# Wider gate-value products, low parts by accumulating transfers, and a shorter end chain in a two-layer decoder trunk on Trainium2

## Chip, cores and metric

The kernel runs on one core of a Trainium2 chip. The metric is the device time of one execution in microseconds (us), as a median over runs. A profile of one execution, taken by the hardware profiler, shows what the core's engines did: TensorE (PE, with its weight loads PEld), VectorE (DVE), ScalarE (ACT), GpSimd (POOL), SyncE (SP), and the transfer (DMA) queues.

## What is computed

Two layers; each adds a mixer and a gated feed-forward to the residual h (512 tokens, width 1024, all in float32). The mixer's input projection yields u and v of a spatial gate and q, k, v of a differential attention. Cut to what matters here:

```python
for l in range(DEPTH):
    n = rmsnorm(h, attn_norm[l])
    u, v_sgu, q, k, v_att = jnp.split(n @ w_in[l], [512, 1024, 1536, 2048], axis=-1)
    u, v_sgu = jax.nn.gelu(u), jax.nn.gelu(v_sgu)
    y_sgu = sgu_mixer(u, v_sgu, ...)   # v normed in 4 groups of 128, mixed over chunks of 128 tokens
    y_att = diff_attention(q, k, v_att, positions, ...)   # 4 heads, rotary on q and k
    h = h + jnp.concatenate([y_sgu, y_att], axis=-1) @ w_out[l]
    h = h + conv_ffn(rmsnorm(h, ffn_norm[l]), ...)        # the larger part of the products
return rmsnorm(h, final_norm)
```

## The kernel before

**Numbers and products.** Every factor of a product is split into a high part (float32 rounded to the type fp32r) and a low part (the value minus its high part, again fp32r). A product is three on TensorE: high x high, high x low, low x high. The activations lie with features on the partitions, 8 tiles of 128 x 512 tokens. `feat_gemm` keeps the weights stationary and moves 512 tokens; its output has features on the partitions. `tok_gemm` keeps 128 tokens stationary and moves weights, 256 columns at a time; its output has tokens on the partitions (the values of the attention and the gate values need this). Two token tiles share a PSUM bank there.

**Weights** come in blocks of 128 x 1024 float32 (512 KB), in a fixed order (`specs`), 96 a layer; of a layer's blocks 0 to 19 are `w_in`: gate values (first half), q of heads 0 and 1, gate values (second half), k, v, q, k, v of the other heads, u. `block(i)` (L156) issues what is needed up to two blocks ahead: a load by SyncE into `raw`, the high part by ScalarE (`act.copy`, L167), the low part by a subtraction (L173), on GpSimd in two halves of 512 columns for the blocks of the mixer after the first seven, on VectorE or GpSimd in the rest. `raw`, `wh` and `wl` have three buffers each.

**Order.** In the mixer the order of instructions on each engine is written out by hand: `Ordered` (L114) chains each instruction to the one before it on its engine. Instructions issued past that wrapper (`nc.sync`, `nc.vector`, `nc.gpsimd`) are set by the planner. The products are generators that yield after each step; `run` takes steps, and after each step one item from the list `due`, in which the work on results is queued (rotary products, gelus, norms, splits).

**Mixer of a layer.** Forty steps come before the attention's loop: in layer 0 gate values and q together as the inputs arrive (`both_first`, 16 steps, from the blocks that `opening` loads piece by piece), the second gate values, k, v; in layer 1 gate values, q, gate values, k, v. Then the loop runs over 16 units (4 heads x 4 query tiles) and two more; each unit has scores, exponentials, difference, transpose, split, product with the values, each some units behind the other, and between these the remaining steps of `products` are run (q, k, v of heads 2 and 3, u). `later` holds items that are done one per unit; in layer 0 these are the last k part, the masks of the spatial weights (`spatial`) and the norm of the second half of the gate values (sums, root, `normed`, `part`). GpSimd does the rotary products of q and k and the subtractions. `rsqrt` is a chain of 11 small VectorE operations.

**PSUM** has four banks for products, two for scores, two for transposes. The gate values of layer 0's second half use the scores' banks.

**End.** The last products (`dl`) run over halves of 256 tokens. For each output tile `squares` adds its square to `acc_last`; `columns` transposes the sums with TensorE, adds them up and takes the root; `result` spreads the roots over the partitions by TensorE into two banks (`sc_last`, copied by ScalarE to `rstd_last` for GpSimd, and `sr_last`, read by VectorE), multiplies and stores by SyncE. The second half's chain stands alone behind the last product.

## Time and profile before

| | |
|---|---|
| median of 3 runs (lowest to highest) | 1132.91 us (1132.48 to 1134.14) |
| profiled execution | 1133.84 us |
| its span, first to last instruction | 1132.1 us |
| TensorE busy | 1115.3 us, 99% |
| VectorE busy | 691.0 us, 61% |
| ScalarE busy | 478.1 us, 42% |
| GpSimd busy | 412.9 us, 36% |
| transfer queue of SyncE | 104.27 MB, 29.1% of 16 engines |

The shares are means over stages: the mixers take about 5 to 205 us and 566 to 759 us of the span, the feed-forwards the rest. A busy TensorE is not one at its peak, since pipelined products overlap in the timeline; the distance from the start of one to the start of the next is what counts. In a row of the timeline or of the groups, `out<-in` are the program's names of the tiles, and what stands behind the last arrow is what ended the idle time before. Nearly all rows have line L119, the wrapper that records every operation, so tiles tell them apart.

### The profile page before, as it was taken

The numbers are of one execution on the slowest core, as the hardware profiler recorded it, in microseconds if no ns is written. First come the engines' busy times: TensorE is split into PE (matmuls) and PEld (weight loads), VectorE is DVE, ScalarE is ACT, GpSimd is POOL, SyncE is SP. The second block draws the span as 40 slices with busy tenths as digits, with TensorE's granted clock in tenths as the row PEclk, the third lists the DMA queues.
The fourth block names the chain that finished last, engine by engine and source line by source line (L and its number), as shares of the span: only waits on it lengthen the run. The fifth ranks groups of instructions, "written<-read, shape, count | busy, mean of one in ns | idle before, by whom it ended". The sixth has DMA issues, their size and how long they took to land.

```text
span 1132.1 us, 14943 instructions
## 1 busy us (share of the span) xinstructions
PE 1115.3 (99%) x5637; PEld 936.4 (83%) x5637; DVE 691.0 (61%) x1271; ACT 478.1 (42%) x810; POOL 412.9 (36%) x390
## 2 busy tenths in 40 slices
PE   9998999999999999999999999999999999999996
PEld 7987888888888888888899788888888888888886
DVE  7779874775763237664347887767657522666634
ACT  6453653544442124443344554454444312444351
POOL 0466233533232103432556742453313310332351
PEclk9999999999999999999999999999999999999999
DMA  8221122232333333223332221122332323322322
GB/s 272 76 79 65 45 65 94 95 101 90 105 94 95 92 112 93 93 84 94 103 110 81 87 74 57 56 94 93 96 109 94 97 91 110 93 94 93 88 80 75
DMA packets 34215, 105.24 MB, mean 93 GB/s; under 512 B 4064, under 2 KB 8544, under 8 KB 34144
## 3 DMA queue, kind: packets, MB, share of 16 engines
q1 hardware_dynamic: 33712, 104.27, 29.1%
q8 instruction: 44, 0.72, 0.3%
q14 instruction: 27, 0.22, 0.1%
q10 hardware_dynamic: 432, 0.03, 0.0%
HBM read 102.19 MB, written 2.10 MB: 92 GB/s over the span
## 4 chain that ended last, share of the span: by engine, by line
PE 87%; DVE 9%; ACT 2%; issue 1%; POOL 1%; DVEq 0%; ACTq 0%; POOLq 0%
PE g L119 21%; PE v L119 20%; PE dn L119 19%; PE wo L119 7%; PE u L119 4%; PE vs L119 3%; PE q L119 3%; PE dl L119 3%; PE av L119 1%; PE sc L119 1%; PE k L119 1%; PE mx L119 1%; DVE s L119 1%; ACT wh L119 1%; PE va L119 1%
## 5 line engine op out<-in xcount | busy, mean ns | idle before, releaser
L119 POOL TENSOR_TENSOR wl<-raw,wh 128x512 fp32r<-128x512 f32 x187 | 256.2, 1391 | 565.1 <-ACT wh L119 546.8
L119 ACT CAST wh<-raw 128x1024 fp32r<-128x1024 f32 (+1 forms) x192 | 194.2, 1015 | 375.7 <-issue 180.3
L119 DVE TENSOR_TENSOR wl<-raw,wh 128x1024 fp32r<-128x1024 f32 (+1 forms) x96 | 121.2, 1263 | 132.1 <-ACT wh L119 132.0
L119 PE MATMUL v<-gh_f,wh 128*128 128x512 f32 x352 | 137.3, 390 | 0.0
L119 PE MATMUL v<-gl_f,wh 128*128 128x512 f32 x352 | 137.0, 389 | 0.0
L119 PE MATMUL v<-gh_f,wl 128*128 128x512 f32 x352 | 137.0, 389 | 0.0
L119 PE MATMUL g<-gh_f,wl 128*128 128x512 f32 x352 | 136.9, 389 | 0.0
L119 PE MATMUL g<-gh_f,wh 128*128 128x512 f32 x352 | 136.9, 389 | 0.0
L119 PE MATMUL g<-gl_f,wh 128*128 128x512 f32 x352 | 136.9, 389 | 0.0
L119 DVE SCALAR_TENSOR_TENSOR cv<-up_cv,par,cv 128x512 f32<-128x512 f32 x88 | 74.0, 885 | 6.4 <-ACT cv L119 6.1
L119 PEld LDWEIGHTS g<-gh_f,wh 128*128 128x128 f32 x352 | 66.1, 188 | 13.8
L119 PEld LDWEIGHTS v<-gh_f,wh 128*128 128x128 f32 x352 | 66.1, 188 | 13.7
L119 PEld LDWEIGHTS v<-gh_f,wl 128*128 128x128 f32 x352 | 66.1, 188 | 13.7
L119 PEld LDWEIGHTS g<-gh_f,wl 128*128 128x128 f32 x352 | 66.1, 188 | 13.7
L119 PEld LDWEIGHTS g<-gl_f,wh 128*128 128x128 f32 x352 | 66.1, 188 | 13.6
L119 PEld LDWEIGHTS v<-gl_f,wh 128*128 128x128 f32 x352 | 66.1, 188 | 13.5
L119 DVE SCALAR_TENSOR_TENSOR cg<-up_cg,par,cg 128x512 f32<-128x512 f32 x88 | 69.6, 841 | 6.0 <-ACT cg L119 5.6
L119 DVE TENSOR_TENSOR up_cv<-v,rstd_f 128x512 f32<-128x512 f32 x44 | 30.2, 692 | 67.2 <-PE v L119 67.2
L119 ACT ACTIVATE s<-s,mn 128x128 f32<-128x128 f32 (+3 forms) x64 | 35.5, 556 | 72.8 <-DVE mn L119 67.5
L119 DVE TENSOR_TENSOR up_cg<-g,rstd_f 128x512 f32<-128x512 f32 x44 | 30.0, 692 | 57.8 <-PE g L119 54.9
L119 DVE TENSOR_TENSOR hT<-dn,hT 128x512 f32<-128x512 f32 x28 | 19.1, 691 | 46.5 <-PE dn L119 46.5
L119 ACT ACTIVATE cg<-cg 128x512 f32<-128x512 f32 x44 | 27.7, 630 | 45.8 <-DVE cg L119 45.8
(604 smaller groups left out, 2618.4 us busy)
## 6 DMA issues: line engine op xcount, KB each, us to landing
raw<-in_w_up SPq DMA_DIRECT2D x88, 512.0 KB, 3.5
raw<-in_w_dn SPq DMA_DIRECT2D x40, 512.0 KB, 3.5
raw<-in_w_in SPq DMA_DIRECT2D x36, 512.0 KB, 3.4
raw<-in_w_out SPq DMA_DIRECT2D x16, 512.0 KB, 3.4
hT<-in_xT SPq DMA_DIRECT2D x8, 256.0 KB, 4.3
or<-in_w_in SPq DMA_DIRECT2D x16, 128.0 KB, 4.4
raw<-in_w_dn SPq DMA_DIRECT2D x8, 256.0 KB, 3.5
out<-y SPq DMA_DIRECT2D x8, 256.0 KB, 2.2
```

Source lines behind the costliest of these rows:

```text
L119: return lambda *args, **kw: pin(getattr(self.engine, op)(*args, **kw))
```

## The change

Three parts.

1. **Gate values.** All 512 columns at once: `tok_wide` moves 512 columns for each token tile, into four banks (two of the scores', two of the products'). The blocks are built from pieces of two old ones. In layer 0 the opening multiplies the gate values alone (its first k in two halves of 256 columns) and q follows as an ordinary product; in layer 1 gate values, then q. The work behind them is done per token tile: gelu, squares and sums, one root over 16 columns for all, `normed`, `part`. Two tiles are normed before the loop, two in it. `spatial` stands ahead of the loop's last 12 steps in both layers, and the rotary products of the first k are put at the front of `due`.
2. **Low parts.** For blocks 10 to 19 of each layer (q, k, v of heads 2 and 3, and u) ScalarE writes the negated high part to `lo` (scale -1, rounded), a transfer issued by GpSimd adds `raw` onto it, and ScalarE writes the high part. The subtractions on GpSimd for these blocks go.
3. **End.** The square of the last tile is transposed by itself; the sum of the others is turned and added up during the last products (k = 7). The bank that VectorE reads is filled before that which ScalarE copies, and stores alternate between SyncE's and ScalarE's queue.

```diff
-        specs += [a["w_in"][l, c] for c in range(20)]
+        w = a["w_in"][l]
+        specs += [[w[c + k // 4][:, k % 4 * 256 : k % 4 * 256 + 512] for c in (0, 4)] for k in range(0, KD, 2)]
+        specs += [w[c] for c in [2, 3] + list(range(6, 20))]
...
     def block(i):
...
+            i_l = j % (len(specs) // DEPTH)
+            if 10 <= i_l < 20:
+
+                act.activation(lo, raw, AF.Identity, scale=-1.0)
+                nc.gpsimd.dma_start(out=lo, in_=raw.bitcast(F32R), accum_op=ALU.add)
+                act.copy(h, raw)
+                loaded.append((h, lo))
+                continue
             act.copy(h, raw)
-            i_l = j % (len(specs) // DEPTH)
             eng = gps if (j > 6 and i_l != 27 if i_l < 28 else j % 3 == 1) else dve
...
+    def tok_wide(banks, xs, ws=None):
+
+        for k, x in enumerate(xs):
+            if ws:
+                w = ws[k]
+            else:
+                if k % 2 == 0:
+                    h, lo = next_block()
+                c = slice(k % 2 * S, k % 2 * S + S)
+                w = h[:, c], lo[:, c]
+            if ws and k == 0:
+
+                for c in (slice(0, 256), slice(256, S)):
+                    outs = [(t, b[:, c], c.start == 0, False) for t, b in enumerate(banks)]
+                    tok_step(outs, x, [p[:, c] for p in w], True, False)
+                    yield
+                continue
+            for t in (0, 2):
+                tok_step([(t + i, banks[t + i], True, True) for i in range(2)], x, w, k == 0, k == len(xs) - 1)
+                yield
...
             if hp == 0:
 
                 later.appendleft(turned.pop())
-                turned = [f for f in turned if f is not nothing]
-            due.extend(turned)
+                due.extendleft(reversed(turned))
+            else:
+                due.extend(turned[:2] + [nothing] * 2 + turned[2:])
...
         def products():
-            if l == 0:
-                yield from both_first()
-                banks = value_banks(1, sc_bank)
-                yield from tok_gemm(banks, xs)
-                g = gate_work(1, banks)
-                due.extend(g[:2])
-                later.extend([lambda: (spatial(), g[2](), g[3]())] + g[4:])
-            else:
-                yield from gate_values(0)
-                yield from queries(0)
-                yield from gate_values(1)
+
+            banks = [sc_bank(f"vs{t}_{l}") for t in range(2)] + [mm_bank(f"vs{t}_{l}") for t in (2, 3)]
+            yield from tok_wide(banks, xs, first if l == 0 else None)
+            gelu, sums, root, normed, part = gate_work(banks)
...
+            due.extend(([nothing] * 4 if l == 0 else []) + [of(gelu, 2, 3), of(gelu, 0, 1)])
+            q = query_banks(0)
+            yield from feat_gemm(q, xs)
+            turn0, turn1, part0, part1 = rope(q, qs, 0, "q")
+            due.extend([turn0, turn1, of(sums, 0, 1), of(sums, 2, 3), part0, part1, root])
+            due.extend(of(f, t) for f in (normed, part) for t in range(2))
+
+            later.extend(of(f, t) for f in (normed, part) for t in (2, 3))
...
-        if l > 0:
-            spatial()
+        spatial()
         run(steps, 12)
...
+        if m == KD - 1 and cs.start > 0:
+            last_sq.append(sq)
+        elif m > 0:
             (dve if m > 5 else gps).tensor_add(acc[:, cs], acc[:, cs], sq)
...
+        if th == 1:
+            s7 = sums("ss_end", last_sq[0])
+            dve.scalar_tensor_tensor(ss, s7, 1.0 / D, ss, op0=ALU.mult, op1=ALU.add)
         act.activation(r, ss, AF.Sqrt)
...
-        for b in (other, bank):
+        for b in (bank, other):
...
-            nc.sync.dma_start(out=out[m : m + 2, :, cs].rearrange("m p s -> p m s"), in_=y.rearrange("p (m s) -> p m s", m=2))
+            (nc.sync if m % 4 == 0 else nc.scalar).dma_start(out=out[m : m + 2, :, cs].rearrange("m p s -> p m s"), in_=y.rearrange("p (m s) -> p m s", m=2))
...
-    products(1, 3, (0,), lambda: r.append(columns(0)))
-    products(1, 3, (1,), lambda: result(0, r[0]))
-    result(1, columns(1))
+    products(1, 3, (0,), {2: lambda: r.append(columns(0, most(0)))})
+    products(1, 3, (1,), {2: lambda: result(0, r[0]), 7: lambda: r.append(most(1))})
+    result(1, columns(1, r[1]))
```

## Rows read from the trace of the kernel before

**Rows 1.** The page: TensorE's busy time, share, instructions; chain by engine.
```profile
PE 1115.3 (99%) x5637; PEld 936.4 (83%) x5637; DVE 691.0 (61%) x1271; ACT 478.1 (42%) x810; POOL 412.9 (36%) x390
...
PE 87%; DVE 9%; ACT 2%; issue 1%; POOL 1%; DVEq 0%; ACTq 0%; POOLq 0%
```
**Rows 2.** Chain that ended last, in order of time: start us, us, what.
```profile
11.89 1.43 PE vs L119 x12
...
250.29 10.88 PE g L119 x48
...
565.81 11.51 PE vs L119 x96
```
**Rows 3.** Waits of TensorE: who for whom, us in total, times, longest us.
```profile
PE av L119 <- DVE or L389: 3.9, 2, 2.8
...
PE at L119 <- DVE aTl L119: 1.1, 2, 1.0
PE sc L119 <- DVE mn L119: 0.5, 1, 0.5
PE sc L119 <- DVE k_0l L119: 0.3, 1, 0.3
```
**Rows 4.** Windows: length, busy PE, PEld, DVE, ACT, POOL, PEclk, DMA share, GB/s.
```profile
90.00:117.00 27.00, 22.77 (x160) 20.11 (x158) 24.93 (x75) 11.76 (x35) 12.63 (x9) 0.94 0.18 59
117.00:142.00 25.00, 25.00 (x155) 20.88 (x155) 21.44 (x74) 14.02 (x44) 8.43 (x6) 1.00 0.14 44
```
**Rows 5.** Timeline of VectorE: start us, us, instruction, idle before and its end.
```profile
109.51 1.24 DVE L384 TENSOR_SCALAR or<-ssq 128x4 int32<-128x4 int32 x1
110.78 0.17 DVE L385 TENSOR_SCALAR ssq<-ssq 128x4 f32<-128x4 f32 x1
...
112.33 0.42 DVE L119 TENSOR_REDUCE o<-av 128x128 f32<-128x256 f32 x1
```
**Rows 6.** Timeline of GpSimd beside it: two low-part subtractions.
```profile
107.68 3.04 POOL L119 TENSOR_TENSOR wl<-raw,wh 128x512 fp32r<-128x512 f32 x2
```
**Rows 7.** Timeline of TensorE: the product behind its longest wait.
```profile
112.89 0.55 PE L119 MATMUL av<-va,aTh 128*128 128x256 f32 x1 [2.77 <-DVE or L389]
```
**Rows 8.** Timeline before the loop of layer 0: ScalarE and TensorE.
```profile
37.92 1.57 ACT L119 ACTIVATE vs<-vs,rcol_a 128x256 f32<-128x256 f32 x4
...
41.88 0.40 PE L119 MATMUL k<-gh_a,wh 128*128 128x512 f32 x1
...
52.79 0.28 PE L119 MATMUL va<-wh,gh_a 128*128 128x256 f32 x1
...
54.98 1.04 ACT L119 CAST wh<-raw 128x1024 fp32r<-128x1024 f32 x1
...
64.88 0.50 PE L119 MATMUL q<-gh_a,wh 128*128 128x512 f32 x1
```
**Rows 9.** The page: groups (busy, mean ns | idle), DMA issues (KB, us to landing).
```profile
L119 POOL TENSOR_TENSOR wl<-raw,wh 128x512 fp32r<-128x512 f32 x187 | 256.2, 1391 | 565.1 <-ACT wh L119 546.8
...
raw<-in_w_in SPq DMA_DIRECT2D x36, 512.0 KB, 3.4
```
**Rows 10.** Timeline: one issue by SyncE; one rotary product on GpSimd.
```profile
10.93 0.43 SPq L119 DMA_DIRECT2D raw<-in_w_in  x1
...
62.88 1.75 POOL L119 TENSOR_TENSOR k_1sh<-k_1sh,sr 128x512 f32<-128x512 f32 x1
```
**Rows 11.** Timeline of VectorE: root of the second half's gate values, layer 0.
```profile
90.02 1.22 DVE L384 TENSOR_SCALAR gr<-gs 128x8 int32<-128x8 int32 x1
```
**Rows 12.** Chain that ended last, behind TensorE's last product.
```profile
1122.81 0.43 DVE acc_last L119
...
1125.97 0.23 PE sr_last L119 x2
```
**Rows 13.** Timeline of the end: GpSimd's and VectorE's last products.
```profile
1126.53 1.41 POOL L119 TENSOR_TENSOR y<-hT,rstd_last 128x256 f32<-128x256 f32 x2 [5.47 <-ACT rstd_last L119]
...
1127.89 0.41 DVE L119 TENSOR_TENSOR y<-hT,sr_last 128x256 f32<-128x256 f32 x1
```

More of the change, by code (lines that the diff above doesn't have):

```diff
@@ L165, in block @@
             lo = wp.tile([P, 1024], F32R, tag="wl", name=f"wl{j}")[:, :n]
-            (sync if j < 6 else nc.sync).dma_start(out=raw, in_=specs[j])
+            queue = sync if j < 6 else nc.sync
+            if wide:
+                for at, half in enumerate(specs[j]):
+                    o = raw.rearrange("p (k i c) -> p i k c", k=2, i=2)[:, at]
+                    queue.dma_start(out=o, in_=half.rearrange("p (k c) -> p k c", k=2))
+            else:
+                queue.dma_start(out=raw, in_=specs[j])
+            i_l = j % (len(specs) // DEPTH)
[5 more added lines that the diff above has]
+                continue
             act.copy(h, raw)
-            i_l = j % (len(specs) // DEPTH)
             eng = gps if (j > 6 and i_l != 27 if i_l < 28 else j % 3 == 1) else dve
@@ L244, in feat_gemm, with tok_step @@
             yield
-    def tok_step(banks, x, w, first, last):
+    def tok_step(outs, x, w, first, last):
         (xh, xl), (h, lo) = x, w
-        for t in range(NT):
+        for t, o, opens, closes in outs:
             ts = slice(t * P, (t + 1) * P)
-            o = banks[t // 2][:, t % 2 * 256 : t % 2 * 256 + 256]
-            mm(o, xh[:, ts], h, start=first and t % 2 == 0, stop=False)
+            mm(o, xh[:, ts], h, start=first and opens, stop=False)
             mm(o, xh[:, ts], lo, start=False, stop=False)
-            mm(o, xl[:, ts], h, start=False, stop=last and t % 2 == 1)
+            mm(o, xl[:, ts], h, start=False, stop=last and closes)
     def tok_gemm(banks, xs):
+        outs = [(t, banks[t // 2][:, t % 2 * 256 : t % 2 * 256 + 256], t % 2 == 0, t % 2 == 1) for t in range(NT)]
         for k, x in enumerate(xs):
@@ L508, in part @@
                 store[at + j] = split(f"{name}{l}_{at + j}", t1[j])
-            return [partial(turn, 0), partial(turn, 1), nothing, nothing, partial(part, 0), partial(part, 1)]
+            return [partial(turn, 0), partial(turn, 1), partial(part, 0), partial(part, 1)]
         later = deque()
@@ L521, in queries @@
             turned = rope(banks, qs, 2 * hp, "q")
-            due.extend(turned if hp else [f for f in turned if f is not nothing])
+            due.extend(turned[:2] + [nothing] * 2 + turned[2:])
         def keys(hp):
@@ L582, in root, with normed, part @@
                 nc.vector.tensor_scalar(gs, gs, 1.0 / P, EPS, op0=ALU.mult, op1=ALU.add)
-                r.append(rsqrt(gs, 8, f"gr{l}_{gp}"))
-            def normed(b):
-                v3 = vts[b].rearrange("p (x d) -> p x d", d=P)
-                rb = r[0][:, 4 * b : 4 * b + 4].unsqueeze(2).to_broadcast([P, 4, P])
+                r.append(rsqrt(gs, NT * NG, f"gr{l}"))
+            def normed(t):
+                v3 = vts[t].rearrange("p (g d) -> p g d", d=P)
+                rb = r[0][:, NG * t : NG * t + NG].unsqueeze(2).to_broadcast([P, NG, P])
                 dve.tensor_tensor(out=v3, in0=v3, in1=rb, op=ALU.mult)
-            def part(b):
-                vg[gp][b] = split(f"vg{l}_{gp}_{b}", vts[b])
-            return [partial(f, b) for f in (gelu, square, sums) for b in range(2)] + [root] + [
-                partial(f, b) for f in (normed, part) for b in range(2)
-            ]
-        def gate_values(gp):
-            banks = value_banks(gp)
-            yield from tok_gemm(banks, xs)
-            g = gate_work(gp, banks)
-            def of(*n):
-                return lambda: [g[i]() for i in n]
-            due.extend([of(0), of(1), of(2, 3), of(4, 5, 6), nothing, nothing, of(7, 8), of(9, 10)])
+            def part(t):
+                vg[t] = split(f"vg{l}_{t}", vts[t])
+            return gelu, sums, root, normed, part
         def gates(c):
@@ L1058, in products, with sums, most, columns @@
             squares(m, cs, H)
[L1060 to L1062 removed]
+    def sums(name, src):
+        bank = tr_bank(name)
         for t in range(2):
[L1064 to L1066 removed]
+            transpose(bank[:, t * P : (t + 1) * P], src[:, t * P : (t + 1) * P], ident)
+        ss = sm.tile([P, 2], F32, tag="ss2", name=name, bufs=3)
+        dve.reduce_sum(ss, bank[:, :H].rearrange("p (t d) -> p t d", t=2), axis=mybir.AxisListType.X)
+        return ss
+    def most(th):
+        ss = sums(f"ss_last{th}", acc[:, th * H : th * H + H])
+        dve.tensor_scalar(ss, ss, 1.0 / D, EPS, op0=ALU.mult, op1=ALU.add)
+        return ss
+    def columns(th, ss):
         t = sm.tile([P, 2], F32, tag="st2", name=f"st_last{th}", bufs=2)
         r = sm.tile([P, 2], F32, tag="sr2", name=f"rcol_last{th}", bufs=2)
[L1069 to L1070 removed]
+        if th == 1:
+            s7 = sums("ss_end", last_sq[0])
+            dve.scalar_tensor_tensor(ss, s7, 1.0 / D, ss, op0=ALU.mult, op1=ALU.add)
         act.activation(r, ss, AF.Sqrt)
```

94 lines of the change are left out of this document (36 added, 58 removed).

## Prediction, before the changed kernel was built or run

> **What bounds the kernel now.** I read the page first: TensorE is busy for 99% of the span, and the chain of work that ended last is 87% TensorE [rows 1]. So a microsecond counts only if it shortens TensorE's products, its waits, or the chain behind its last product. Second, the pitch of the products, from the chain of waits in order of time [rows 2]: twelve 256-column products take 1.43 us (119.2 ns each), forty-eight of 512 columns 10.88 us (226.7 ns each). Durations in the timeline overlap, so the pitch is the price. Third, TensorE's waits [rows 3]: outside start and end only 5.8 us, all in the attention loops (3.9 + 1.1 + 0.5 + 0.3). Fourth, the windows [rows 4]: in 90 to 117 us TensorE is busy 22.77 of 27 us and VectorE 24.93, and the granted clock is 0.94, which is some microseconds at the lower of the two levels (1.2 GHz) after TensorE had stood idle: 27 x 0.06 = 1.6 us of work lost. In 117 to 142, where VectorE has 21.44 of 25, TensorE does not wait at all. Fifth, who holds VectorE up [rows 5 to 7]: an operation on a 128x4 tile takes 0.17 us at 110.78, and one like it 1.24 us at 109.51, just while GpSimd subtracts low parts (107.68 to 110.72). VectorE waits out a GpSimd operation. Behind them stands the reduction of o at 112.33, which frees the PSUM bank, and TensorE's longest wait (2.77 us) ends on it at 112.89.
>
> **Part 1, gate values as products of 512 columns.** Layer 1: two groups of 96 products at 11.51 us each [rows 2] are 23.02 us; 96 products of 226.7 ns are 21.76 us: -1.26 us. Layer 0: 192 x 119.2 ns = 22.9 us; the new order keeps 24 products of 256 columns for the first k and has 84 of 512, 2.86 + 19.04 = 21.9 us: -1.0 us. All on the path, since TensorE is paced by its own products there. Sum -2.2 us; bounds -2.4 and -1.8, as start-up might eat part of layer 0.
>
> The gate values now hold two banks of the scores' pool and two of the products' pool. The keys' products need the latter freed by the gelus of tokens 2 and 3. In before the gelus (four of 256) begin on ScalarE at 37.92 us and take 1.57 us [rows 8]; two of 512 columns should be over by about 39.2, and the keys, at 41.88 now, would start 1 us earlier. This is near enough to allow 0 to 0.5 us of a new wait per layer; I take 0.3 us for both together. ScalarE's pieces get fewer (4 gelus for 8), the squares and sums stay as many.
>
> **Part 2, the low parts of ten blocks a layer.** Removed: for blocks 10 to 19 of a layer two GpSimd subtractions of 1391 ns [rows 9], 20 x 2.8 = 56 us of GpSimd that is off the path. Added: on ScalarE one pass over 128x1024 for each block, about the 1.0 us of the cast [rows 8], 20 us in all; one transfer of 512 KB from SBUF to SBUF, issued on GpSimd's queue. Neither issue nor transfer is in this trace. The issue is bounded by SyncE's 0.43 us [rows 10] and the 2.8 us that it replaces; I take 1.4. The transfer is bounded by the 3.4 us of a 512 KB load [rows 9] and three times that (two operands read, one written): 10.2 us; I take 6.8, as two passes.
>
> What hides it is the lead of two blocks. Block 10's conversion may start when the keys' last product ends and the values' first begins, 52.79 us; TensorE reads block 10 at 64.88 [rows 8]: 12.1 us. Less 1.0 for the negation and 1.4 for the issue this leaves 9.7 us for the transfer, so 6.8 is hidden and 10.2 would cost 0.5 us a layer. (Its cast starts at 54.98 now, behind the normed gate values in ScalarE's order; in the new order these stand behind it.) Later blocks are read over attention units and have more lead. Queued behind the issue on GpSimd, which waits for ScalarE's negation as the subtraction waited for the cast, are the rotary products of q and k; they go first-in first-out as before and start some 1.4 us earlier. The issue is not part of the hand-written order, so the planner might set it elsewhere on that queue. If the cover is gone, TensorE waits for the rest of the transfer, block by block.
>
> ScalarE's 1.0 us more in front of the exponentials: in 90 to 117 it is busy 11.76 of 27 us, in 117 to 142 14.02 of 25 [rows 4]; four to six more microseconds leave it at about 60 to 65%. I price the delays at 0.5 us of wait, inside the remainder below (0 to 2 us).
>
> **Where the waits go.** Three things relieve VectorE in the loops. First, the subtractions are gone: in front of TensorE's longest wait at least 1.07 us of VectorE's delay (1.24 against 0.17) lies under one of them, and the rotary products, which queue behind such subtractions on GpSimd, move forward. Second, in layer 0 sums and root of the second half of the gate values leave the loop; there one of their operations took 1.22 us [rows 11], and the waits of 1.1 and 0.5 us stand behind them. Third, the keys' rotary comes three steps earlier (the 0.3). VectorE's own work in 90 to 117 then falls to about the 21.4 of 25 at which TensorE does not wait. At stake are 5.8 + 1.6 = 7.4 us; bounds 0 and -7.4; I take -5.2, two thirds, because the rotary products on GpSimd stay and still block VectorE, and ScalarE gets its 0.5. In front of the loop VectorE gets two sums more and the root, some 4 us, where TensorE has no wait.
>
> The Trainium skill has the lock behind this: "SBUF — State Buffer", § Who interferes with whom, says that a VectorE instruction with two SBUF inputs contends with a GpSimd instruction that reads SBUF, and that the loser blocks entirely. The trace agrees (1.24 us for 0.17). The same page, § SBUF: two separate sides, speaks against this change: a transfer issued by GpSimd has its descriptors written by GpSimd's cores, which a VectorE operation in a two-port mode locks out. No run here shows it yet; it is rival 3. By "DMA: Bandwidth & Descriptors", § Anatomy of one DMA — SWDGE (gpsimd) path, an estimate for 512 KB is 2.0 + 1.2 = 3.2 us; the sum would be the same, as both are hidden.
>
> **Part 3, the end.** The last square is no longer added to the running sum (-0.45 us with its gap) and the bank that VectorE reads is filled before the other (-0.23 us) [rows 12]; two transposes move in front of the last products (+0.23 us, the price of such a pair in the chain). VectorE's last product ends at 1128.30 [rows 13] and would end at 1127.85; GpSimd's, fed by the bank that is now second, ends at 1127.94 in both and is late next. So -0.4 us; bounds +0.2 and -0.5. Stores on two issuing queues bring nothing: the last store waits for data, not for its queue.
>
> **Sum.** -2.2 + 0.3 - 5.2 - 0.4 = -7.5 us. The profiled execution took 1133.84 us (span 1132.1 and 1.7 around it), 0.9 above the median of the runs; a difference of 7.5 against the median of 1132.91 gives **1125.4 us**.
>
> **Rivals.**
> 1. The waits stay, because VectorE is full even without the subtractions (24.93 of 27 us) and the rotary products take their place as blockers. Against it: 117 to 142. It leaves parts 1 and 3: 1132.9 - 2.2 + 0.3 - 0.4 = 1130.6; with a fifth of the waits gone, 1129.1. I put it at 1130.
> 2. Slower: the transfer takes longer than the 9.7 us that hide it at block 10. An accumulating transfer may run at a fraction of a load's rate; nothing in this trace shows one. At five loads' time (17 us) TensorE waits 7.3 us in each layer and loses 1.6 us of clock after each wait, as it does now after its longest: +17.8 - 7.5 gives 1143. From 10 us on it decides, from about 13.5 us on the time is above before's. For it: the unknown rate. Against it: a load of 512 KB lands in 3.4 us [rows 9].
> 3. The issue on GpSimd is held up by VectorE. As a mechanism here: beside VectorE's work a GpSimd product takes 1.75 us [rows 10] where the subtractions of that size take 1.39 in the mean; an issue that meets several VectorE operations might take 3 to 5 us, the transfer would come 2 to 3.5 us later, and at 6.8 us block 10 would be about on time, at 10.2 some 3 us late in each layer, and the rotary products behind the issue as late as now: half of the gain of the waits (2.6) goes: about 1128 to 1130, say 1129. The rule of the Trainium skill's "SBUF — State Buffer", § SBUF: two separate sides, named above, is this rival's.
>
> **How the numbers follow.** Forecast 0.70 (its own range 1122.5 to 1128.5: waits between all and a third removed, and the bounds of parts 1 and 3), rival 1 0.13, rival 2 0.10, rival 3 0.07. The range reaches down to the case in which all waits go (1122.9, rounded to 1122) and up over rivals 1 and 3 to 1131.5; rival 2 and the tails are left out. A measurement of this kernel can tell about 0.2% (2.3 us) from no change; below 1130.6 are nearly all of the forecast, most of rivals 1 and 3: faster 0.81; same 0.10 (rest of rival 1, mild forms of 2); slower 0.09.
>
> **What would show it.** Part 1: the gate values' products 96 in a layer at a pitch near 227 ns, layer 1's stretch 21.8 us. Part 2: no low-part subtraction on GpSimd between the rotary products; a queue of GpSimd's with some 20 transfers; TensorE's waits in the loops under 2.5 us and the granted clock at 1.00 through 90 to 117; VectorE's 128x4 and 128x8 operations near 0.17 us. Part 3: last store 0.4 us earlier behind TensorE's last product. The forecast is wrong if TensorE waits for a transfer, if ScalarE becomes what VectorE and TensorE wait for in the loops, or if VectorE's busy share there does not fall.

## The result, and the profile after

The changed kernel takes 1123.96 us (median of five, 1123.66 to 1124.32) against 1132.91 before (median of five, 1132.13 to 1135.08); the ratio is 0.9917, its 95% interval 0.9904 to 0.9931. The forecast was 1125.4 in a range of 1122.0 to 1131.5: the direction held and so did the chief mechanism, the subtractions that hold VectorE; the gain is 1.4 us larger than said. The profiled execution of the changed kernel took 1124.22 us with a span of 1122.5.

The page of the changed kernel, with the lines that answer to rows 1 and 9: TensorE's busy line, the subtractions that stay on GpSimd, the transfers (KB each, median us from issue to landing) and their queue.

```profile
PE 1110.7 (99%) x5459; PEld 925.3 (82%) x5459; DVE 674.1 (60%) x1242; ACT 494.3 (44%) x814; POOL 374.8 (33%) x370
...
q0 software_dynamic: 2880, 10.49, 4.8%
...
L119 POOL TENSOR_TENSOR wl<-raw,wh 128x512 fp32r<-128x512 f32 x147 | 201.9, 1394 | 515.8 <-ACT wh L119 515.7
...
wl<-raw POOLq DMA_DIRECT2D x20, 512.0 KB, 4.6
```

There are 20 transfers, and 40 fewer subtractions on GpSimd (147 for 187). The page lists no wait, so the next view is TensorE's waits, which answers to [rows 3]:

```profile
PE sr_last L119 <- DVE rcol_last L119: 1.8, 1, 1.8
PE idle L119 <- DVE zeros L136: 1.3, 1, 1.3
PE ss_end L119 <- DVE sq L119: 1.1, 1, 1.1
PE at L119 <- DVE aTl L119: 1.0, 2, 0.6
```

The first and the third are the end, the second is the start; rows of 0.3 us and less at the start and in the feed-forward are left out. In the attention loops 1.0 us is left of 5.8, and the longest single wait is 0.6 us where it was 2.8. The windows of the two loops (length; busy PE, PEld, DVE, ACT, POOL; granted clock; DMA share; GB/s), two for layer 0 and two for layer 1; the second of each pair ends with the loop, as 90 to 117 us does in [rows 4]:

```profile
63.00:83.00 20.00, 20.00 (x104) 15.18 (x103) 14.30 (x48) 14.17 (x31) 5.42 (x6) 1.00 0.77 198
83.00:110.00 27.00, 26.56 (x192) 22.97 (x191) 24.64 (x73) 18.36 (x46) 10.66 (x10) 1.00 0.58 143
614.00:634.00 20.00, 20.00 (x104) 15.15 (x103) 14.29 (x48) 13.89 (x29) 5.40 (x7) 1.00 0.82 196
634.00:661.00 27.00, 26.45 (x192) 22.85 (x190) 24.65 (x74) 18.29 (x48) 10.94 (x10) 1.00 0.58 144
```

In the 27 us that end with layer 0's loop TensorE is busy 26.56 us where it was 22.77, with 192 recorded products for 160, and the granted clock is 1.00, the higher of its two levels. VectorE's share is hardly lower: 24.64 us for 24.93. What fell is its time over the whole loop. Before, the first half of layer 0's loop reads

```profile
64.00:90.00 26.00, 25.82 (x135) 19.57 (x135) 19.34 (x53) 13.85 (x35) 18.12 (x16) 1.00 0.25 81
```

so VectorE spent 19.34 + 24.93 = 44.3 us there, and spends 14.30 + 24.64 = 38.9 now, 5.3 us less. In layer 1's loop it spent 40.3 us and spends 38.5. VectorE's timeline in the changed kernel shows the operations that GpSimd held in [rows 5] at their own length, 0.17 us where one took 1.24:

```profile
102.14 0.17 DVE L423 TENSOR_SCALAR or<-ssq 128x4 int32<-128x4 int32 x1
102.35 0.17 DVE L424 TENSOR_SCALAR ssq<-ssq 128x4 f32<-128x4 f32 x1
...
105.00 0.42 DVE L119 TENSOR_REDUCE o<-av 128x128 f32<-128x256 f32 x1
```

Where the time went is seen best from TensorE's timeline: the start of the first product of each step in both kernels, and how far the changed one is ahead by then.

| first product of | before, us | after, us | ahead, us |
|---|---|---|---|
| keys, layer 0 | 41.88 | 40.76 | 1.12 |
| scores, layer 0 (loop begins) | 64.39 | 63.24 | 1.15 |
| gates u, layer 0 (loop nearly over) | 116.90 | 109.62 | 7.28 |
| gate values, layer 1 | 565.65 | 558.38 | 7.27 |
| keys, layer 1 | 600.55 | 591.95 | 8.60 |
| scores, layer 1 | 623.06 | 614.43 | 8.63 |
| gates u, layer 1 | 670.61 | 660.96 | 9.65 |
| last product of the kernel | 1121.58 | 1112.01 | 9.57 |
| end of the span | 1132.12 | 1122.50 | 9.62 |

So layer 0's loop gave 6.1 us, layer 1's 1.0, the gate values 1.1 and 1.3, the end next to nothing. (The profiled execution of before lay 0.9 us above its median, which is why this table ends at 9.6 and the medians differ by 8.95: executions of before lie near 1132.3 us with a mean granted clock of 0.997 or 0.998, near 1133.8 with 0.995 or 0.996, and near 1135.2 with 0.993 or 0.994, so not each of them loses the clock that the profiled one lost.)

### The profile page after: what moved, and what is told of

It is laid out like the page before. It is cut to its first block, busy times and chain, and to the rows that moved or that the text cites. A ratio compares the mean times of both kernels' runs of the same rounds, so it can differ in the third digit from the quotient of the medians.

```text
span 1122.5 us, 14572 instructions
## 1 busy us (share of the span) xinstructions
PE 1110.7 (99%) x5459; PEld 925.3 (82%) x5459; DVE 674.1 (60%) x1242; ACT 494.3 (44%) x814; POOL 374.8 (33%) x370
## 3 DMA queue, kind: packets, MB, share of 16 engines
q0 software_dynamic: 2880, 10.49, 4.8%
## 4 chain that ended last, share of the span: by engine, by line
PE 88%; DVE 6%; ACT 3%; issue 1%; POOL 1%; DMA 0%; SPq 0%; POOLq 0%; DVEq 0%; ACTq 0%
PE g L119 21%; PE v L119 21%; PE dn L119 19%; PE wo L119 7%; PE u L119 4%; PE vs L119 4%; PE dl L119 2%; PE va L119 2%; PE q L119 2%; PE av L119 1%; PE sc L119 1%; PE mx L119 1%; DVE s L119 1%; PE k L119 1%; ACT wh L119 1%
## 5 line engine op out<-in xcount | busy, mean ns | idle before, releaser
L119 POOL TENSOR_TENSOR wl<-raw,wh 128x512 fp32r<-128x512 f32 x147 | 201.9, 1394 | 515.8 <-ACT wh L119 515.7
```

The source lines that it names most:

```text
L119: return lambda *args, **kw: pin(getattr(self.engine, op)(*args, **kw))
```

## The experiments

Times are medians; "over" and "under" are against the changed kernel's 1123.96 us unless before is named. The kernel before ran again beside each group of experiments, with medians of 1133.35 to 1133.95 us; the changed kernel did not. Kernels that share their opening begin the keys of layer 0 anywhere between 40.05 and 40.86 us, so differences of some tenths of a microsecond between medians are not read as effects.

**The transfers undone, and the transfers alone.** First the changed kernel with GpSimd's subtractions back:

```
-            if 10 <= i_l < 20:
+            if False:
```

> The changed kernel with the transfers taken out again: GpSimd subtracts the low parts of blocks 10 to 19 as in the kernel before; gate products, order of the waiting work and end stay as changed. Theory (the subtractions on GpSimd made the waits in the attention loops): most of the 7.3 us that the loops lost come back, 1128.5 to 1131.5 us. Rival (the new order did it: gelus and root of the gate values out of the loops, less for VectorE to do there): under 1 us comes back, 1124 to 1125 us. A time between says how the gain is shared.

Measured: 1136.08 us (1134.95 to 1137.87), 12.1 over, and slower than before: ratio 1.0021 (1.0013 to 1.0030). This is outside what either theory said. Then the opposite, the kernel before with the transfers as its only change:

```
+            i_l = j % (len(specs) // DEPTH)
+            if 10 <= i_l < 20:
+                act.activation(lo, raw, AF.Identity, scale=-1.0)
+                nc.gpsimd.dma_start(out=lo, in_=raw.bitcast(F32R), accum_op=ALU.add)
+                act.copy(h, raw)
+                loaded.append((h, lo))
+                continue
             act.copy(h, raw)
-            i_l = j % (len(specs) // DEPTH)
```

> The kernel before with the transfers alone: blocks 10 to 19 get the negated high part by ScalarE and the transfer that adds onto it; gate products of 256 columns, old order, old end. Theory: the loops of both layers lose their 7.3 us or nearly, the rest stays: 1125.5 to 1127.5 us. Rival (the root, normalisation and splits that the old order leaves in the loops keep the waits): 1129 to 1132 us.

Measured: 1126.74 us (1126.47 to 1126.98), ratio to before 0.9939 (0.9926 to 0.9951), about 7 us. The transfers by themselves bring nearly all that the loops gain. The rest of the change, without them, costs time. By loop, from the first product of the scores to the first of the gates u, with VectorE's busy time in it:

| kernel | layer 0, us | VectorE | layer 1, us | VectorE |
|---|---|---|---|---|
| before | 52.5 | 43.8 | 47.6 | 40.3 |
| before with the transfers alone | 46.7 | 38.2 | 46.4 | 35.7 |
| changed, subtractions back | 52.0 | 46.2 | 53.2 | 47.4 |
| changed | 46.4 | 38.3 | 46.5 | 38.5 |

With the transfers in place the new order changes the loops by -0.3 and +0.1 us. The kernel with the transfers alone still has the sums, the root and the norm of the second half of the gate values in layer 0's loop, so that work was no bar once the subtractions were gone. In layer 1 the transfers took 4.6 us off VectorE and TensorE gained only 1.1: there TensorE had hardly waited for it.

Where the new order costs time is seen in the kernel with the subtractions back, at the start of layer 0's loop: VectorE, GpSimd, then TensorE.

```profile
63.67 1.78 DVE L119 TENSOR_TENSOR vg_0l<-vs,vg_0h 128x512 fp32r<-128x512 f32 x1
65.38 1.77 DVE L119 TENSOR_TENSOR vg_1l<-vs,vg_1h 128x512 fp32r<-128x512 f32 x1
...
63.16 3.44 POOL L119 TENSOR_TENSOR wl<-raw,wh 128x512 fp32r<-128x512 f32 x2
...
68.61 0.59 PE L119 MATMUL sc<-k_0h,q_0h 64*128 64x256 f32 x2 [1.21 <-DVE mn L119]
```

The new order puts the splits of the gate values right ahead of the loop. Under a subtraction each takes 1.78 us instead of 0.68 (its length in the kernel with dead writes below), the loop's first maxima (mn) come late, and TensorE waits 1.21 us; layer 1 shows the same (1.29). The loss is in layer 1's loop, 5.6 us over before; layer 0's is 0.5 us shorter than before. The new order pays only together with the transfers.

**Is it the reading, or the work?** Two kernels leave the transfers in place and add work to GpSimd whose results nobody reads (dead work). One brings the subtractions back:

```
                 act.copy(h, raw)
+                for c in (slice(0, 384), slice(384, 768), slice(768, 1024)):
+                    gps.tensor_sub(dead[:, : c.stop - c.start], raw[:, c], h.bitcast(F32)[:, c])
```

> The changed kernel with the subtractions of blocks 10 to 19 back on GpSimd as dead work: three pieces (384, 384 and 256 columns) from the same tiles, written to a scratch tile that nobody reads, beside the transfers that still make the low parts. So GpSimd holds VectorE up as before, but no product waits for it. Theory (VectorE's work behind GpSimd's reads makes the waits): most of the 7.3 us come back, 1128 to 1131 us. Rival (it was the late low parts themselves, GpSimd's queue ending after the product wanted them): about 1124 to 1125 us.

Measured: 1150.96 us (1150.90 to 1151.00), 27 over. The other fills the same place with writes:

```
                 act.copy(h, raw)
+                for _ in range(7):
+                    gps.memset(dead, 0.0)
```

> The changed kernel with dead work on GpSimd that fills about the same time and reads nothing: seven writes of zeros, 128x384, into a scratch tile for each of blocks 10 to 19. Theory (VectorE is held by GpSimd's operations on two inputs, not by GpSimd being busy): under +0.6 us, 1124.0 to 1124.6. Rival (a busy GpSimd delays the splits, rotary parts and the transfers' issue behind it, and that made the waits): +2 to +6 us, 1126 to 1130.

Measured: 1124.32 us (1124.05 to 1124.56), not to be told from the changed kernel. The timelines of VectorE and GpSimd side by side, first with dead subtractions:

```profile
64.81 1.95 DVE L119 TENSOR_TENSOR vg_0l<-vs,vg_0h 128x512 fp32r<-128x512 f32 x1
66.68 1.50 DVE L119 TENSOR_TENSOR vg_1l<-vs,vg_1h 128x512 fp32r<-128x512 f32 x1
...
64.90 3.86 POOL L119 TENSOR_TENSOR dead<-raw,wh 128x384 fp32r<-128x384 f32 x3
```

and with dead writes:

```profile
63.23 0.68 DVE L119 TENSOR_TENSOR vg_0l<-vs,vg_0h 128x512 fp32r<-128x512 f32 x1
64.00 0.69 DVE L119 TENSOR_TENSOR vg_1l<-vs,vg_1h 128x512 fp32r<-128x512 f32 x1
...
62.70 3.27 POOL L119 MEMSET dead<- 128x384 f32 x7
```

The windows from 86 to 97 us of both (columns as above), dead subtractions first, show GpSimd nearly full in either:

```profile
86.00:97.00 11.00, 11.00 (x61) 8.70 (x62) 10.93 (x25) 7.90 (x20) 10.61 (x10) 1.00 0.52 123
```

```profile
86.00:97.00 11.00, 10.66 (x70) 8.95 (x69) 10.38 (x27) 7.44 (x20) 9.77 (x19) 1.00 0.59 152
```

No product reads the dead results, and TensorE waits for no transfer and no cast in this kernel, so a late low part is not the cause. A GpSimd that only writes, nearly as busy, leaves VectorE's splits at 0.68 us. It is GpSimd's reading beside VectorE that held VectorE and through it TensorE. (Shown for operations that read two tiles; one that reads a single tile was not tried.) The rule of the Trainium skill that the prediction used ("SBUF — State Buffer", § Who interferes with whom) also says that a GpSimd instruction which only writes SBUF does not contend; both traces agree, 1.95 against 0.68 us. The prediction's own row for that rule (1.24 for 0.17 us) is no instance of its two-input case: that operation (`or<-ssq`) reads one tile and was held all the same; a split reads two (`vs` and `vg_0h`). The size was missed by far, 27 us for the expected 4 to 7. The two loops are 13.3 and 12.9 us longer. TensorE's waits for VectorE in them add up to 18.7 us (o alone ends two of 5.2, one in each loop), and the mean granted clock is 0.988 for 0.997, by an estimate from these two 0.009 x 1149 = 10 us. Why dead subtractions cost 15 us more than the real ones of the kernel with the subtractions back was not taken apart; they come in three pieces, and ScalarE's pass and the transfers run on top of them.

**VectorE in GpSimd's place.** If the hold is the harm, VectorE could subtract these blocks itself:

```
-            if 10 <= i_l < 20:
+            if False:
...
-            eng = gps if (j > 6 and i_l != 27 if i_l < 28 else j % 3 == 1) else dve
+            eng = gps if (j > 6 and i_l != 27 and not 10 <= i_l < 20 if i_l < 28 else j % 3 == 1) else dve
```

> The changed kernel with the low parts of blocks 10 to 19 subtracted by VectorE, 128x1024 at 1.26 us each, in place of the transfers: nothing is left for GpSimd to read there, so VectorE is not held, but it has 1.26 us more work a block. Theory (the transfers pay because VectorE has no room in the loops: 22.7 us busy of 27 in layer 0's second stretch, where some five blocks would add 6.3): VectorE becomes the bound, +2 to +7 us over the changed kernel, 1126 to 1131. Rival (the hold by GpSimd was all the harm, and VectorE's own work fits into its gaps): 1124 to 1125.

Measured: 1131.08 us (1130.76 to 1131.39), 7.1 over and 0.26% under before. So the same subtractions cost 1136.1 us on GpSimd, 1131.1 on VectorE, 1124.0 as transfers: of the 12.1 us between first and last, 5.0 go when the work moves to VectorE, although VectorE then has to do it, and 7.1 when VectorE is rid of it too. (The 22.7 of 27 us in the expectations was read over 88 to 115 us, past the end of the loop; inside it VectorE is fuller, 24.64.) TensorE's waits with VectorE subtracting, the first two rows in the loops, the last right behind them:

```profile
PE at L119 <- DVE aTl L119: 2.9, 2, 1.5
PE at L119 <- DVE s L119: 1.9, 4, 0.8
...
PE ot L119 <- DVE cf L717: 1.5, 2, 0.8
```

**The root back in the loop.** The order's share, with the transfers in place:

```
-            due.extend([turn0, turn1, of(sums, 0, 1), of(sums, 2, 3), part0, part1, root])
-            due.extend(of(f, t) for f in (normed, part) for t in range(2))
-
-            later.extend(of(f, t) for f in (normed, part) for t in (2, 3))
+            due.extend([turn0, turn1, of(sums, 0, 1), nothing, part0, part1])
+            later.extend([of(sums, 2, 3), root])
+            later.extend(of(f, t, t + 1) for t in (0, 2) for f in (normed, part))
```

> The changed kernel with the sums of the last two gate tiles, the root and all of the normalisations and splits moved back into the attention loop, one a turn. The rest as changed. Theory (with the subtractions off GpSimd the loop has room): 0 to +0.7 us, 1124.0 to 1124.7. Rival (the loop's waits came from this work, VectorE's 23 of 27 us in the stretch leave no room for 10 us more): +2 to +5 us, 1126 to 1129.

Measured: 1128.43 us (1128.13 to 1129.10), 4.5 over: my theory falls, the rival holds. The 27 us that end with layer 0's loop, and the wait that came:

```profile
85.00:112.00 27.00, 24.61 (x179) 21.30 (x177) 24.65 (x72) 16.86 (x42) 9.21 (x9) 1.00 0.47 120
```

```profile
PE av L119 <- DVE o L119: 3.0, 2, 1.5
```

VectorE is as full as in the changed kernel (24.65 of 27 us for 24.64) and GpSimd no fuller, but TensorE loses 2.4 us of this window instead of 0.4, as the reduction of o comes behind the gate values' work. The share doesn't show the wait; the order of the work makes it. So a loop that is free of the subtractions still has no room for the gate values' whole work in this order; the loops grow to 48.7 us each. It is not the price of what the kernel before kept there (the second half's sums, root and norm, in layer 0 alone): with the transfers alone that loop holds it in 46.7 us, 0.3 more than the changed kernel's.

**One block ahead.** Does the lead hide the transfer?

```
-        while len(loaded) <= min(i + AHEAD[0], len(specs) - 1):
+        ahead = lambda j: min(AHEAD[0], 1) if 10 <= j % (len(specs) // DEPTH) < 20 else AHEAD[0]
+        while len(loaded) <= min(i + ahead(len(loaded)), len(specs) - 1):
```

> The changed kernel with blocks 10 to 19 prepared one block ahead of use in place of two. Theory (the transfer is hidden by the lead of two blocks, not by being short): ScalarE's pass 1.0 us, issue 0.87 and landing 4.6 make 6.5 us, one block of 24 products at 226.7 ns lasts 5.4 us and 6 to 8 with the attention's work between: 0 to 1 us of wait a block, +2 to +10 us in all, 1126 to 1134. Rival (the lead does not matter; ScalarE and the queue run early enough anyway): under +0.6, 1124.0 to 1124.6.

Measured: 1133.10 us (1130.92 to 1134.09), 9.1 over, all of the gain. GpSimd's issue, TensorE's product behind it and the window around them, layer 0:

```profile
62.86 1.01 POOL L182 DMA_DIRECT2D wl<-raw  x1
...
67.46 0.50 PE L119 MATMUL q<-gh_a,wl 128*128 128x512 f32 x1 [2.90 <-DMA wl<-raw]
```

```profile
64.00:75.00 11.00, 8.10 (x32) 5.83 (x32) 5.81 (x23) 7.11 (x17) 0.86 (x1) 0.84 0.67 144
```

Only block 10 is late, once in each layer (2.90 and 2.84 us), not every block as I had it. Behind that wait some of the time is at the lower level (1.2 GHz): the granted clock is 0.84 over these 11 us, by an estimate 0.16 x 11 = 1.8 us of work. The loops last 50.5 and 51.4 us, 4.1 and 4.9 more than in the changed kernel. This is rival 2 of the prediction in a small form.

**The width alone.** The gate values in pieces of 256 columns again, everything else as changed:

```
             for t in (0, 2):
-                tok_step([(t + i, banks[t + i], True, True) for i in range(2)], x, w, k == 0, k == len(xs) - 1)
+                for c in (slice(0, 256), slice(256, S)):
+                    outs = [(t + i, banks[t + i][:, c], c.start == 0, c.start > 0) for i in range(2)]
+                    tok_step(outs, x, [p[:, c] for p in w], k == 0, k == len(xs) - 1)
```

> The changed kernel with the products of the gate values in 256 columns again, in the new order and with everything else as changed. Theory (width alone is part 1): 192 pairs of 256 columns in place of 192 products of 512 less the first step of layer 0, which was narrow already: by the rows of the kernel before, 2 x 119.2 - 226.7 = 11.7 ns a product, +1.1 us in layer 0's 84 wide ones of 96 and +1.1 in layer 1's 96: 1126.0 us (1125.6 to 1126.3). Rival (part 1's 1.15 and 1.36 us came from the order, not the width): 1124.0 to 1124.6.

Measured: 1126.04 us (1125.71 to 1126.60), 2.1 over. The chain in order of time has the first stretch of layer 1's gate values, 60 wide products in the changed kernel and 120 narrow ones here:

```profile
558.54 13.60 PE vs L119 x60
```

```profile
559.68 14.39 PE vs L119 x120
```

13.60 / 60 = 226.7 ns and 14.39 / 120 = 119.9 ns, the pitches of [rows 2] within 0.7 ns. (In the expectations layer 0's 84 products should read 1.0 us; 1.1 is for 96.)

**The end.** The end of the kernel before in the changed kernel (one sum of eight squares behind the last product, its order of banks, and all stores on SyncE's queue; the edit is cut to its main lines):

```
-            s7 = sums("ss_end", last_sq[0])
-            dve.scalar_tensor_tensor(ss, s7, 1.0 / D, ss, op0=ALU.mult, op1=ALU.add)
...
-        for b in (bank, other):
+        for b in (other, bank):
...
-    products(1, 3, (1,), {2: lambda: result(0, r[0]), 7: lambda: r.append(most(1))})
-    result(1, columns(1, r[1]))
+    products(1, 3, (1,), lambda: result(0, r[0]))
+    result(1, columns(1))
```

> The changed kernel with the end of the kernel before: one sum over all eight squares after the last product, no separate last square. Theory (the trace: the chain ahead of the scale got 0.46 us shorter, and TensorE's clock, at the lower level before the last four transposes, took it back; the two transposes put in cost 0.2 ahead of the last product): the old end costs -0.3 to +0.1, 1123.7 to 1124.1 us. Rival (the shorter chain is worth the 0.4 us of the prediction): +0.3 to +0.5, 1124.3 to 1124.5.

Measured: 1124.20 us (1124.14 to 1124.52), 0.24 over, which the medians can't tell from nothing. By the traces the stretch from the start of the last product to the end lasts 10.49 us in the changed kernel, 10.54 in the one before, and 11.29 here. The last two run the same end; 0.45 us of their difference is the clock, at which the last transposes run, and the rest lies behind the last product of the result. TensorE's timeline at the end of the changed kernel, and a window over it:

```profile
1112.01 0.28 PE L119 MATMUL dl<-ac_21h,wl 128*128 128x256 f32 x1
1113.35 0.41 PE L119 MATMUL ss_end<-ident,sq 128*128 128x128 f32 x2 [1.07 <-DVE sq L119]
1115.59 0.66 PE L119 MATMUL sr_last<-ident,rcol_last 128*128 128x128 f32 x2 [1.83 <-DVE rcol_last L119]
1116.04 0.64 PE L119 MATMUL sc_last<-ident,rcol_last 128*128 128x128 f32 x2
```

```profile
1115.00:1118.00 3.00, 1.09 (x4) 0.72 (x4) 2.08 (x9) 0.37 (x1) 0.78 (x2) 0.50 0.01 2
```

After two idle stretches (1.07 and 1.83 us) the granted clock is 0.50, the lower level, and the last transposes take 0.66 and 0.64 us. That is not a property of this end. The kernel with dead writes has the same end and the same waits, and its transposes run at the higher level:

```profile
1115.51 0.41 PE L119 MATMUL sr_last<-ident,rcol_last 128*128 128x128 f32 x2 [1.82 <-DVE rcol_last L119]
```

Of the nine traces with the changed end and no dead products in it, four have these transposes at the lower level (0.66 us) and five at the higher (0.40 or 0.41); of the three with the old end, two and one. So two ends are to be compared at the same level. From the start of TensorE's last product to the end of the last product of the result it is 6.7 us in the kernel before and 6.2 with dead writes, both at the higher level, and 7.2 here and 6.6 in the changed kernel at the lower: the changed end is 0.5 to 0.6 us shorter at either. The span ends 3.6 to 4.1 us later, at a point that moves by 0.26 us between traces with equal rows up to there, and the two transposes put in cost some 0.1 us ahead of the last product. To hold the clock, dead products of zeros were put into these gaps:

```
         if th == 1:
+            keep(4)
             s7 = sums("ss_end", last_sq[0])
             dve.scalar_tensor_tensor(ss, s7, 1.0 / D, ss, op0=ALU.mult, op1=ALU.add)
+        if th == 1:
+            keep(7)
         act.activation(r, ss, AF.Sqrt)
...
+    def keep(n):
+        bank = sc_bank(f"keep{n}")
+        for _ in range(n):
+            mm(bank, zeros[:, :P], zeros, start=True, stop=True)
```

> The changed kernel with dead products of zeros into a spare bank where TensorE waits at the end: four ahead of the last two sums' transposes, seven ahead of the last four transposes (0.21 us each at the higher clock, so 0.9 and 1.5 us within waits of 1.1 and 1.8). Theory (the clock that fell at 1115.0 us takes the end's gain): the four transposes go at the higher level, 0.4 in place of 0.66 and 0.64 us for the first, -0.3 to -0.6 us: 1123.4 to 1123.7. Rival (the clock is no matter there, or the dead products come in the way): -0.1 to +0.6.

Measured: 1123.71 us (1123.56 to 1124.18). The last transposes in this kernel, and its clock:

```profile
1115.24 0.40 PE L119 MATMUL sr_last<-ident,rcol_last 128*128 128x128 f32 x2 [0.31 <-DVE rcol_last L119]
1115.48 0.38 PE L119 MATMUL sc_last<-ident,rcol_last 128*128 128x128 f32 x2
```

```profile
1115.00:1116.00 1.00, 0.62 (x4) 0.41 (x4) 0.41 (x2) 0.04 (x1) 0.00 (x0) 1.00 0.00 0
```

The transposes run at the higher level (0.40 for 0.66 us), but they do so in five traces without dead products too, and these end as early behind the last product (9.98 to 10.25 us for 10.26 here). So it is not shown that the dead products held the clock, nor that they are worth the 0.25 us by which the median is lower; the medians can't tell it from nothing.

**A wider last stretch.** The down products of feature blocks 4 and 5 over 512 tokens (`whole`), and with it the first half's sums at step 9 of its stretch, as its inputs come later (cut to the calls):

```
-        products(0, c, (0, 1))
-    products(1, 2, (0, 1))
+        if c == 2:
+            whole(c)
+        else:
+            products(0, c, (0, 1))
...
-    products(1, 3, (0,), {2: lambda: r.append(columns(0, most(0)))})
+    products(1, 3, (0,), {9: lambda: r.append(columns(0, most(0)))})
```

> The changed kernel with the down products of output blocks 4 and 5 (the last stretch's first pair) over 512 tokens in place of twice 256, and the first half's sums taken at step 9 instead of step 2 of the next stretch but one. Theory (TensorE sets the pace to the end): 60 products at 2 x 119.2 - 226.7 = 11.7 ns less, -0.7 us, and nothing is late behind it: 1123.1 to 1123.5. Rival (the first half's sums, taken later, push its result onto the second half's work): 0 to +1, 1124 to 1125.

Measured: 1124.05 us (1123.64 to 1124.27): no gain. TensorE's waits name the reason:

```profile
PE sr_last L119 <- DVE rcol_last L119: 2.6, 2, 1.8
```

The changed kernel has 1.8 us on this row, once; the second wait, 0.8 us, is for the first half's scale, which now comes too late, and it is as long as the 0.7 us that were to be gained. Both ideas together:

> The dead products at the end and the wider down products together. If both hold they add up: -1.0 to -1.3 us, 1122.7 to 1123.0. If the end's order spoils either: no less than the better of the two alone.

Measured: 1123.84 us (1123.70 to 1124.05), no better than the dead products alone; the new wait is there again (0.8 us).

## Why the prediction came out as it did

**Part 1 (-2.2 forecast; right).** Undoing the width costs 2.1 us. The trace has 1.1 us in layer 0 and 1.3 in layer 1 for the terms of -1.0 and -1.26; layer 0's is the softer number, as the keys' start differs by up to 0.8 us between kernels with the same opening.

**The new wait of the keys (+0.3 forecast; absent).** The gelus ran from 36.82 us for 2.42 us, over at 39.24, where the prediction put 39.2; the keys began at 40.76 without a wait in either layer. The bound of 0 was the right end.

**Part 2, what hides the transfer (right, with less to spare than it seemed).** The issue is bounded in the prediction by 0.43 and 2.8 us, taken as 1.4; the group of the 20 issues on GpSimd gives 0.87 in the mean:

```profile
L181 POOL DMA_DIRECT2D wl<-raw x20 | 17.4, 870 | 62.1 <-ACT wl L119 62.1
```

The transfer, taken as 6.8 us between 3.4 and 10.2, lands in 4.6 (median). The estimate by the Trainium skill ("DMA: Bandwidth & Descriptors", § Anatomy of one DMA — SWDGE (gpsimd) path) was 3.2 us; 4.6 was measured, and that decides. But block 10's, the one that has the least cover, takes 7.0 us in both layers; the view of its issue in layer 0 shows the load issued beside it, and the second view a transfer that has no load beside it, issued at 96.61 us:

```profile
wl<-raw POOLq DMA_DIRECT2D x1, 512.0 KB, 7.0
raw<-in_w_in SPq DMA_DIRECT2D x1, 512.0 KB, 4.4
```

```profile
wl<-raw POOLq DMA_DIRECT2D x1, 512.0 KB, 4.4
```

Of the 20 transfers the ten that share less than 2 us of their flight with loads land in 4.4 to 4.6 us, the two that share 4.4 us in 7.0. So 6.8 us was about right for the block that counts, and the median flatters. Block 10's issue came at 55.28 us, later than the 52.79 plus 1.0 of the prediction, because GpSimd was still at block 9's subtractions; with 7.0 us it lands at 62.2, and TensorE first reads it at 64.29. About 2 us of cover are left. With one block of lead the issue comes at 62.86 instead of 55.28, and TensorE waits 2.9; the kernel before with the transfers alone waits 0.4 us once:

```profile
PE q L119 <- DMA wl<-raw: 0.4, 1, 0.4
```

So the cover is real and not large, and rival 2 was the right thing to fear.

**Where the waits go (-5.2 forecast; about -7.2 between the two profiled executions, some 0.9 less against before's median).** This is the term that was mis-sized. Of the stake of 5.8 us of waits and 1.6 of clock the prediction took -5.2 (0.7 of it; two thirds would be 4.9), because the rotary products stay on GpSimd and still block VectorE, and ScalarE gets more work. The first is true, but it costs less than that: beside a rotary product of the changed kernel an operation of VectorE takes 1.87 us that takes 0.75 without one, and the wait of 0.44 us behind it is one of the two that are left; the other (0.55) follows the same operation in layer 1. VectorE twice, then GpSimd and TensorE:

```profile
84.84 1.87 DVE L119 SCALAR_TENSOR_TENSOR s<-s,cf,s 128x512 f32<-128x512 f32 x1
...
108.06 0.75 DVE L119 SCALAR_TENSOR_TENSOR s<-s,cf,s 128x512 f32<-128x512 f32 x1
...
84.86 1.29 POOL L119 TENSOR_TENSOR q_3t<-q_3t,q_3sh 128x512 f32<-128x512 f32 x1
...
87.23 0.66 PE L119 MATMUL at<-ident,s 128*128 128x128 f32 x4 [0.44 <-DVE aTl L119]
```

ScalarE, 18.36 of 27 us, is named in none of TensorE's waits. The waits left are 1.0 us, and no clock is lost in the loops. That makes 4.8 + 1.6 = 6.4; some 0.7 of the 7.2 us by which the loops got shorter I can assign to no row. The three reasons given for this term fare differently. The subtractions: shown, by dead reads against dead writes and by the transfers alone, which bring 5.8 and 1.1 of the 6.1 and 1.0 us. The root out of the loop, and the keys' rotary part three steps earlier: the kernel with the transfers alone has neither, and its loops are 0.3 us longer and 0.1 us shorter, so the two, with the rest of the new order, are worth next to nothing there once the subtractions are gone. That the forecast came within 1.4 us is in part luck: it counted on two reasons that gave nothing, and it left 2.2 us of the stake for holds and for ScalarE, of which the holds took 1.0 and ScalarE nothing. What the prediction missed besides is that the parts are not a sum: without the transfers the new order costs 4.5 us (1.0021 x 1133.8 is 2.4 above before, although the width still gives 2.1), with them it is worth about 0.7 together with the end (1126.74 - 1123.96 less the width's 2.1).

**Part 3 (-0.4 forecast; -0.05 between the two profiled executions, -0.5 to -0.6 at the same clock level, less 0.1 ahead of the last product).** The shorter chain is there: the second sum's transposes start 1.34 us behind the start of the last product where they started 1.80 behind it. The step that failed is the price of the four transposes behind it, which were taken at the durations of before (0.23 us a pair): in before's trace the clock fell only after them, at 1126.5, in the changed kernel's before them, and the same operations took 0.66 and 0.64. Which of the two happens differs between traces with the same end, so the -0.05 is chance, and the medians (0.24 us for the old end) are too close to tell.

**Rivals.** Of 1 (VectorE stays full, so the waits stay) the premise held and the conclusion not: VectorE is at 24.64 of 27 us for 24.93, and the waits are gone. My own argument against it, that VectorE would fall to the share of 117 to 142 us, was wrong too, and so was the sign that I named, a falling busy share: what falls is VectorE's time per loop (5.3 us in layer 0), since the loop shrinks with it. 2 (the transfer is late) did not happen and was made to happen; its limit of 13.5 us leaves out the 1.6 us of clock per layer that its own sum counts, and with them it is 11.9. 3 (GpSimd's issue held by VectorE) is not seen: the 20 issues take 0.85 to 1.03 us each, and the transfer issued at 102.64 us, with VectorE busy during all of its flight, lands in 4.6. The rule of the Trainium skill that it was taken from ("SBUF — State Buffer", § SBUF: two separate sides) shows in no row here.

## What to carry to other kernels

Where TensorE waits for VectorE, look at what GpSimd reads at that moment: VectorE's operation there may be short work held for long, and then moving GpSimd's work onto a queue can pay although GpSimd itself is far from full. Try the parts of such a change by themselves; here the new order was a loss without the transfers and changed the loops by 0.3 us at most with them. An engine's busy share is a poor sign: VectorE stayed at nine tenths in the loop with and without TensorE's waits, while its time in layer 0's loop fell by 5.3 us and TensorE gained 6.1. Nor does freed time pay by itself: the transfers alone took 4.6 us off VectorE in layer 1's loop, and TensorE gained 1.1. A transfer that replaces an engine's work needs its cover counted from the real start of its issue and with the landing time of the one transfer that has the least of it, not the median; one block less of lead can cost all of the gain.

## What the runs showed of the hardware that was not expected

- A GpSimd that only writes (9.8 of 11 us busy) cost VectorE nothing that can be measured (38.3 us busy in layer 0's loop with and without); one that reads two tiles in each operation (10.6 of 11 us) cost the kernel 27 us.
- A transfer from SBUF to SBUF that adds onto its target moved 512 KB in 4.6 us in the median, only 1.2 above the 3.4 of a plain load; beside a load, with 4.4 us of common flight, it took 7.0. Its issue occupied GpSimd for 0.87 us, less than one of the two subtractions that it replaces.
- At the end of the kernel, with the same gaps in TensorE's work, the last transposes ran at the lower clock level in some traces and at the higher in others (six each of the twelve without dead products). A change of tenths of a microsecond there can only be read between traces at the same level.
